# Half the tokens' expert gates by scatter-add into a DRAM grid instead of one-hot matmuls

## The chip, the cores and the metric

The kernel runs on one core of a Trainium2 chip. The metric is the device time of one execution in microseconds, the median of several runs.

## The reference

Two blocks in a row work on 256 tokens of width 1024, all in float32. The first is two layers of sparse attention, short convolution and a squared-ReLU MLP. The second has windowed and neighbourhood attention, and then PEER, the part that the change touches. It retrieves single-neuron experts by product keys:

```python
qh = (xc @ w_query).reshape(PEER_CHUNK, PEER_HEADS, PEER_QDIM)
s1 = einsum('thd,hnd->thn', qh[..., :128], sub_keys[:, 0]); s2 = ... # second half
v1, i1 = top_k(s1, 16); v2, i2 = top_k(s2, 16)
cand = v1[..., :, None] + v2[..., None, :]          # 256 candidates
vs, ci = top_k(cand, 16)
e1 = i1[ci // 16]; e2 = i2[ci % 16]; idx = e1 * 128 + e2
g = softmax(vs)
z = einsum('td,thkd->thk', xc, u_experts[idx])
y = einsum('thk,thkd->td', gelu(z) * g, v_experts[idx])
```

There are 8 heads and 128 x 128 = 16,384 experts.

## The kernel before

The kernel computes PEER densely: it multiplies all 256 tokens by all 16,384 rows of u, masks the gelu with the gates (zero where an expert was not chosen), and multiplies by all rows of v. An expert number is e1 * 128 + e2. A *block* is the 128 experts with one e2; e1 is the partition. The tile `big` (128 partitions x 128 blocks x 256 tokens, 128 KB a partition) holds gelu and gate, first the one and then their product.

A float32 product is made of three float32r products: each weight block is split into a high part (ScalarE, L88) and a low part (VectorE, L89), and TensorE multiplies high by high, high by low and low by high (L117 to L119, L353 to L355). The class `Stream` loads each 512 KB block on SP's queue (L76) into one of three raw buffers, three blocks ahead in PEER (six in the layers), and splits it two blocks ahead (four in the layers).

PEER has three stages:

1. *Up-projection with selection* (L997 to L1009). 24 matmuls per block (`up`, L901); gelu goes into `big` (L911). At blocks 0, 9, ..., 63 a head's query is made with two more weight blocks (`query`, L922), and the generator `select` (L941) takes the scores through top-16, candidates, top-16 and the look-up of e1 and e2 on VectorE. `select` yields after each piece; per block the loop takes SEL_RATE = 1.3 pieces, and three more per query. After all heads the softmax of vs is made and e1, e2 and g are transposed to eT, with tokens along the free dimension (L987 to L991).
2. *Up-projection with gates* (L1038 to L1049). For every four tokens `onehots` makes two 128 x 512 comparisons on VectorE (L1020) and scales the second by g on ScalarE (L1023); `gates` multiplies them on TensorE (L1029, one matmul per token, two records each), which sums the heads and gives 128 x 128 gates of a token. Where gelu is already in `big`, VectorE multiplies it by them (L1031); for the blocks to come ScalarE stores the gates (L1033), and `up` multiplies gelu into them later (L908, L909). The groups of all 256 tokens are spread over the rest of the blocks but the last two (LEAD).
3. *Value* (L1063 to L1079). Pairs of blocks of `big` are split (L124), and 12 matmuls of 512 columns per block add them times v into four PSUM tiles. Then comes the tail, with the residual, the final norm and the output.

The order of the instructions on each engine is planned by the library's scheduler: what is ready goes first, by program order among what is ready, as it reckons the times; `issue_after` and `manual_schedule` fix it by hand. An engine's queue is then worked off in that order, and an instruction that waits holds what is behind it. The DMA queue of SP carries the weights, that of POOL (GpSimd) the small tables, the sub-keys (L924) and row broadcasts (L348). The MLP of the first layer (L659 to L673) is touched too.

Of the kernel before, what the change touches and what calls it, by code (L numbers as in the profile page):

```python
# [9 lines left out]
F32 = mybir.dt.float32  # L10
# [33 lines left out]
GB = 3  # L44
TURN = 1
# [10 lines left out]
SEL_RATE = 1.3  # L56
# [468 lines left out]
def layer(k, l, stream, x, u, rs):  # L525
# [114 lines left out]
    with k.tc.tile_pool(name="mlp", bufs=1, reuse_waits="tile") as mlp:  # L640
# [18 lines left out]
        for j in range(0, HID // P, 2):  # L659
# [52 lines left out]
def ada_steps(k, pool, j0, j1, after):  # L712
# [181 lines left out]
def peer(k, x, pool, hp, stream, u):  # L894
    nc = k.nc
    a = k.a
    with ExitStack() as es:
        eT = pool.tile([P, 3, T], F32, name="eT")
        big = es.enter_context(k.tc.tile_pool(name="bigp", bufs=1, reuse_waits="tile")).tile([P, P, T], F32, name="big")

        def up(e2, done, gl):  # L901
# [4 lines left out]
            if done:  # L906
                g = gl.tile([P, T], F32, name="gl", tag="gl", bufs=2)
                nc.scalar.activation(g[:, :done], ps[:, :done], AF.Gelu_apprx_tanh)  # L908
                nc.vector.tensor_tensor(out=big[:, e2, :done], in0=g[:, :done], in1=big[:, e2, :done], op=ALU.mult)  # L909
            if done < T:  # L910
                nc.scalar.activation(big[:, e2, done:], ps[:, done:], AF.Gelu_apprx_tanh)  # L911
            return end

        e2 = 0
        with k.tc.tile_pool(name="tk", bufs=1, reuse_waits="tile") as tk:
            io16 = tk.tile([P, PK], F32, name="io16")
            nc.gpsimd.dma_start(out=io16, in_=a["iota"][:, :PK])
            vs = [tk.tile([P, H, PK], F32, name=f"vs{t}") for t in range(NT)]
            eg = [tk.tile([P, 3, H * PK], F32, name=f"eg{t}") for t in range(NT)]
# [21 lines left out]
            def select():  # L941
                for h in range(H):
                    while h not in scores:
                        yield
                    s = scores.pop(h)
                    for t in range(NT):
                        v12 = tk.tile([P, 2, PK], F32, name="v12", tag="v12", bufs=2)
                        i12 = tk.tile([P, 2, PK], U32, name="i12", tag="i12", bufs=2)
                        for c in range(2):
                            top16(k, s[:, t, c, :], v12[:, c, :], i12[:, c, :])  # L950
                            yield
                        if12 = tk.tile([P, 2, PK], F32, name="if12", tag="if12", bufs=2)
                        nc.vector.tensor_copy(out=if12, in_=i12)
                        cand = tk.tile([P, PK, PK], F32, name="cand", tag="cand", bufs=1)
                        nc.vector.tensor_tensor(out=cand, in0=v12[:, 0, :, None].to_broadcast([P, PK, PK]),
                                                in1=v12[:, 1, None, :].to_broadcast([P, PK, PK]), op=ALU.add)
                        yield
                        vi = tk.tile([P, PK], U32, name="vi", tag="vi", bufs=2)
                        top16(k, cand.rearrange("p a b -> p (a b)"), vs[t][:, h, :], vi)
                        yield  # L960
                        ab = tk.tile([P, 2, PK], U32, name="ab", tag="ab", bufs=2)
                        nc.vector.tensor_scalar(out=ab[:, 0, :], in0=vi, scalar1=4, scalar2=None,
                                                op0=ALU.logical_shift_right)
                        nc.vector.tensor_scalar(out=ab[:, 1, :], in0=vi, scalar1=15, scalar2=None, op0=ALU.bitwise_and)
                        abf = tk.tile([P, 2, PK], F32, name="abf", tag="abf", bufs=2)
                        nc.vector.tensor_copy(out=abf, in_=ab)
                        for c in range(2):
                            eq = tk.tile([P, PK, PK], F32, name="eq", tag="cand", bufs=1)
                            nc.vector.tensor_tensor(out=eq, in0=abf[:, c, :, None].to_broadcast([P, PK, PK]),
                                                    in1=io16[:, None, :].to_broadcast([P, PK, PK]), op=ALU.is_equal)  # L970
                            nc.vector.tensor_tensor(out=eq, in0=eq, in1=if12[:, c, None, :].to_broadcast([P, PK, PK]),
                                                    op=ALU.mult)
                            nc.vector.tensor_reduce(out=eg[t][:, c, h * PK:(h + 1) * PK], in_=eq, axis=AX.X,
                                                    op=ALU.add)
                            yield
                for t in range(NT):
                    g = eg[t][:, 2, :].rearrange("p (h k) -> p h k", h=H)
                    nc.vector.tensor_tensor(out=g, in0=vs[t], in1=vs[t][:, :, 0:1].to_broadcast([P, H, PK]),
                                            op=ALU.subtract)
                    nc.scalar.activation(g, g, AF.Exp)  # L980
                    den = k.small.tile([P, H], F32, name="den", tag="den")
                    nc.vector.tensor_reduce(out=den, in_=g, axis=AX.X, op=ALU.add)
                    nc.vector.reciprocal(out=den, in_=den)
                    nc.vector.tensor_tensor(out=g, in0=g, in1=den[:, :, None].to_broadcast([P, H, PK]), op=ALU.mult)
                    yield
                    yield
                    ps = k.psm.tile([P, 4, P], F32, name="pst", tag="m")  # L987
                    with k.tc.issue_after(k.end):
                        for c in range(3):
                            nc.tensor.transpose(ps[:, c, :], eg[t][:, c, :], k.ident)  # L990
                    nc.scalar.activation(eT[:, :, t * P:(t + 1) * P], ps[:, 0:3, :], AF.Copy)  # L991
                    yield
# [18 lines left out]
        with k.tc.tile_pool(name="gs", bufs=1, reuse_waits="tile") as gs:  # L1011
            iota = gs.tile([P, P], F32, name="iota")
            nc.gpsimd.dma_start(out=iota, in_=a["iota"])
# [24 lines left out]
            while e2 < P:  # L1038
                upto = min(T, -(-T * (e2 - start + 1) // (P - start - LEAD)))
# [10 lines left out]

            gf = hp.tile([P, 2, D], F32, name="gf", tag="h2hi")
# [30 lines left out]
            xg = gs.tile([P, 512], F32, name="xg", tag="o1", bufs=GB)  # L1082
# [40 lines left out]
def body(tc, a):  # L1123
# [3 lines left out]
    with ExitStack() as es:  # L1127
# [17 lines left out]
        k.t5one = dram.tile([H, 512], F32, name="t5one")  # L1145
        k.ada = keep.tile([P, 48], F32, name="ada")
# [147 lines left out]
```

## Time and profile before

| | |
|---|---|
| median of 3 runs | 1733.88 us (1733.78 to 1741.08) |
| profiled execution | 1734.41 us, span 1732.5 us |
| TensorE busy | 1696.7 us, 98% of the span |
| VectorE, ScalarE, POOL busy | 75%, 52%, 5% |
| moved by DMA | 328.87 MB, 190 GB/s over the span |
| TensorE's granted clock | full in all 40 slices |

A span is the time from the first to the last instruction on the core; the execution's own time has 1.9 us around it. Matmuls overlap, so the mean of one (about 283 ns) is not what one costs; that is read from how many run in a stretch.

### The profile page before, as it was taken

To read this page: it belongs to the slowest core of one execution; us is meant where nothing else is said; L and a number is where in the kernel's file an instruction comes from. 1 tells how busy PE (TensorE), PEld (TensorE's weight loads), DVE (VectorE), ACT (ScalarE), POOL (GpSimd) and SP (SyncE) were. 2 spreads that over 40 slices of the span, in tenths; PEclk is the share of its full clock that TensorE was granted. 3 is DMA by queue.
4 is the path that set the end of the run, shared out by engine and by line. 5 is a ranking of instruction groups with operands and counts; after the bars stand their busy time and mean duration, and the time that the engine had idled before them with its cause. 6 is when DMAs were issued, how large, how long until landed. Compare 5 with 4: busy or idle time off the path is not lost.

```text
span 1732.5 us, 29333 instructions
## 1 busy us (share of the span) xinstructions
PE 1696.7 (98%) x11365; PEld 1557.2 (90%) x11365; DVE 1305.3 (75%) x2131; ACT 902.3 (52%) x1550; POOL 82.3 (5%) x109
## 2 busy tenths in 40 slices
PE   8999999999999999999999999999999999999997
PEld 7899899887999998888789999999999888888886
DVE  6867788766867878767678788799999855555555
ACT  6544544345544544354444444478877644444443
POOL 1000000000000000036100000000000000000000
PEclk9999999999999999999999999999999999999999
DMA  8445667965455659874145655654444566666664
GB/s 309 147 148 183 218 202 242 370 228 195 140 165 183 224 184 318 314 235 150 52 143 181 192 171 185 188 170 123 135 126 124 176 195 190 190 192 193 190 190 131
DMA packets 90778, 328.87 MB, mean 190 GB/s; under 512 B 10384, under 2 KB 10496, under 8 KB 90256
## 3 DMA queue, kind: packets, MB, share of 16 engines
q1 hardware_dynamic: 88144, 318.33, 56.9%
q0 software_dynamic: 2496, 8.68, 1.5%
q8 instruction: 89, 1.46, 0.3%
q14 instruction: 49, 0.40, 0.1%
HBM read 325.88 MB, written 3.19 MB: 190 GB/s over the span
## 4 chain that ended last, share of the span: by engine, by line
PE 90%; DVE 6%; ACT 1%; issue 1%; DMA 1%; SPq 0%; POOLq 0%; POOL 0%; ACTq 0%; DVEq 0%
PE pw L117 15%; PE pw L118 15%; PE pw L119 15%; PE acc L355 13%; PE acc L354 13%; PE acc L353 13%; PE pst L1029 2%; DVE big L1031 2%; DVE wlo L89 1%; DVE o L1020 1%; PE po L473 1%; PE pst L171 1%; PE pst L465 1%; PE sc L812 1%; ACT whi L88 1%
## 5 line engine op out<-in xcount | busy, mean ns | idle before, releaser
L88 ACT ACTIVATE whi<-raw 128x1024 fp32r<-128x1024 f32 (+1 forms) x549 | 572.9, 1048 | 572.8 <-PE pw L118 276.2
L89 DVE TENSOR_TENSOR wlo<-raw,whi 128x1024 fp32r<-128x1024 f32 (+1 forms) x549 | 669.2, 1222 | 253.4 <-ACT whi L88 251.5
L117 PE MATMUL pw<-h2hi,whi 128*128 128x256 f32 x1152 | 331.2, 288 | 0.1
L118 PE MATMUL pw<-h2lo,whi 128*128 128x256 f32 x1152 | 326.0, 283 | 0.3 <-DVE h2lo L178 0.3
L119 PE MATMUL pw<-h2hi,wlo 128*128 128x256 f32 x1152 | 325.8, 283 | 0.0
L117 PE MATMUL pw<-uhi,whi 128*128 128x256 f32 x1000 | 284.9, 285 | 0.0
L119 PE MATMUL pw<-uhi,wlo 128*128 128x256 f32 x1000 | 284.1, 284 | 0.0
L118 PE MATMUL pw<-ulo,whi 128*128 128x256 f32 x1000 | 284.1, 284 | 0.0
L118 PEld LDWEIGHTS pw<-h2lo,whi 128*128 128x128 f32 x1152 | 221.1, 192 | 0.5 <-DVE h2lo L178 0.5
L117 PEld LDWEIGHTS pw<-h2hi,whi 128*128 128x128 f32 x1152 | 220.8, 192 | 0.7 <-ACT big L911 0.5
L119 PEld LDWEIGHTS pw<-h2hi,wlo 128*128 128x128 f32 x1152 | 220.9, 192 | 0.0
L355 PE MATMUL acc<-whi,al 128*128 128x512 f32 x512 | 201.8, 394 | 0.0
L354 PE MATMUL acc<-wlo,ah 128*128 128x512 f32 x512 | 200.7, 392 | 0.0
L353 PE MATMUL acc<-whi,ah 128*128 128x512 f32 x512 | 198.8, 388 | 0.3 <-ACT ah L124 0.3
L118 PEld LDWEIGHTS pw<-ulo,whi 128*128 128x128 f32 x1000 | 192.3, 192 | 1.3 <-issue 1.3
L117 PEld LDWEIGHTS pw<-uhi,whi 128*128 128x128 f32 x1000 | 192.4, 192 | 0.9 <-issue 0.7
L119 PEld LDWEIGHTS pw<-uhi,wlo 128*128 128x128 f32 x1000 | 192.2, 192 | 0.7 <-issue 0.7
L354 PEld LDWEIGHTS acc<-wlo,ah 128*128 128x128 f32 x512 | 96.1, 188 | 22.5
L353 PEld LDWEIGHTS acc<-whi,ah 128*128 128x128 f32 x512 | 96.1, 188 | 21.9 <-ACT ah L124 0.5
L355 PEld LDWEIGHTS acc<-whi,al 128*128 128x128 f32 x512 | 96.3, 188 | 19.5 <-DVE al L124 0.4
L353 PE MATMUL acc<-whi,hhi 128*128 128x512 f32 x256 | 99.9, 390 | 0.0
L354 PE MATMUL acc<-wlo,hhi 128*128 128x512 f32 x256 | 99.8, 390 | 0.0
(253 smaller groups left out, 2495.0 us busy)
## 6 DMA issues: line engine op xcount, KB each, us to landing
raw<-in_w_layers_dram SPq DMA_DIRECT2D x240, 512.0 KB, 4.3
raw<-in_u_dram SPq DMA_DIRECT2D x128, 512.0 KB, 3.7
raw<-in_v_dram SPq DMA_DIRECT2D x128, 512.0 KB, 4.3
aw<-in_w_ada_dram SPq DMA_DIRECT2D x48, 512.0 KB, 5.9
raw<-in_w_query_dram SPq DMA_DIRECT2D x16, 512.0 KB, 3.6
raw<-in_w_qkb_dram SPq DMA_DIRECT2D x8, 512.0 KB, 5.4
raw<-in_w_out_dram SPq DMA_DIRECT2D x8, 512.0 KB, 3.6
raw<-in_w_idx_dram SPq DMA_DIRECT2D x8, 324.0 KB, 6.3
```

Source lines behind the costliest of these rows:

```text
L88: self.nc.scalar.activation(hi[:, :w], r[:, :w], AF.Copy)
L89: self.nc.vector.tensor_sub(lo[:, :w], r[:, :w], hi[:, :w])
L117: nc.tensor.matmul(out, a[0], b[0], start=first, stop=False)
L118: nc.tensor.matmul(out, a[0], b[1], start=False, stop=False)
L119: return nc.tensor.matmul(out, a[1], b[0], start=False, stop=last).ins
L171: k.nc.tensor.transpose(ps[:, c, :], src[:, (c0 + c) * P:(c0 + c + 1) * P], k.ident)
L353: nc.tensor.matmul(acc, a[0], w[0][:, o:o + cols], start=first, stop=False)
L354: nc.tensor.matmul(acc, a[0], w[1][:, o:o + cols], start=False, stop=False)
L355: return nc.tensor.matmul(acc, a[1], w[0][:, o:o + cols], start=False, stop=last).ins
L465: nc.tensor.transpose(ps[:, i, :], sm[:, h, c * P:(c + 1) * P], k.ident)
L1029: nc.tensor.matmul(ps[:, i, :], o1[:, i, :], o2[:, i, :], start=True, stop=True)
L1031: nc.vector.tensor_tensor(out=b[:, :, :cur], in0=ps[:, :, :cur], in1=b[:, :, :cur], op=ALU.mult)
```

## The change

Tokens 0 to 127 keep the one-hot matmuls, now 32 groups of four instead of 64, over the blocks after the selection. For tokens 128 to 255 the gates take another way:

- A DRAM grid `gscr` of 128 x 128 x 128 floats (e1, e2, token; 8.4 MB) is cleared by 16 DRAM-to-DRAM writes of 512 KB, listed one per pair of blocks in the first layer's MLP.
- `select` works on both token tiles at once, makes the softmax after each pair of heads, and works out each gate's place e1 * 16384 + e2 * 128 + token. Then `add_gates` issues 16 indirect DMAs a head from POOL, each adding one gate per token, 128 floats, to the grid. The DMAs of a head don't wait for each other; those of the next head wait for all of them.
- In the value stage `gated_pair` loads the grid four blocks at a time (256 KB, SP) and multiplies a pair of blocks of `big` by it on VectorE, two pairs ahead; the first grid loads wait for the last head's DMAs. The split of a pair is listed one pair ahead, in two buffers instead of three.
- The sub-keys and two tables are loaded on SP's queue instead of POOL's; SEL_RATE is 1.25 instead of 1.3, without the three extra pieces per query.

```diff
+SB = 2
+GQ = 4
+ZERO = 4096
-SEL_RATE = 1.3
+SEL_RATE = 1.25
...
+            if l == 0:
+                clear(k, j // 2, HID // P // 2)
...
+def clear(k, i, n):
+    piece = k.gscr.rearrange("(n r c) o -> n r (c o)", n=n, c=ZERO)[i]
+    k.nc.sync.dma_start(out=piece, in_=k.a["zeros"].to_broadcast(list(piece.shape)))
...
-            if done < T:
-                nc.scalar.activation(big[:, e2, done:], ps[:, done:], AF.Gelu_apprx_tanh)
+            nc.scalar.activation(big[:, e2, done:], ps[:, done:], AF.Gelu_apprx_tanh)
...
+        def add_gates(h):
+            now = []
+            for j in range(PK):
+                ins = nc.gpsimd.indirect_dma_start(
+                    out=k.gscr, out_offset=bass.IndirectOffsetOnAxis(ap=place[:, h, j:j + 1], axis=0),
+                    in_=gate[:, h, j:j + 1], in_offset=None, compute_op=ALU.add).ins
+                k.tc.declare_no_dep(ins, group=f"gates{h}", reason="a head's experts differ, and so do the tokens")
+                k.tc.add_to_no_dep_group(f"gates{h}", ins)
+                for p in added:
+                    k.tc.add_manual_dep(ins, p.name, order, reason="heads add one after the other")
+                now.append(ins)
+            added[:] = now
...
-                keys = tk.tile([P, 2, P], F32, name="keys", tag="keys", bufs=1)
-                nc.gpsimd.dma_start(out=keys, in_=a["sub_keys"][:, 2 * h:2 * h + 2, :])
+                keys = tk.tile([P, 2, P], F32, name="keys", tag="keys", bufs=2)
+                nc.sync.dma_start(out=keys, in_=a["sub_keys"][:, 2 * h:2 * h + 2, :])
...
+                    at = tk.tile([P, PK], F32, name="at", tag="at", bufs=2)
+                    nc.vector.tensor_scalar(out=at, in0=en[:, 1, 1], scalar1=float(P), scalar2=slot, op0=ALU.mult,
+                                            op1=ALU.add)
+                    nc.vector.scalar_tensor_tensor(out=at, in0=en[:, 0, 1], scalar=float(P * P), in1=at, op0=ALU.mult,
+                                                   op1=ALU.add)
+                    nc.vector.tensor_copy(out=place[:, h, :], in_=at)
+                    if h % 2:
...
+                        nc.scalar.activation(e, e, AF.Exp)
...
+                        for i in (h - 1, h):
+                            add_gates(i)
...
-                    due += 3
...
-                upto = min(T, -(-T * (e2 - start + 1) // (P - start - LEAD)))
+                upto = min(P, -(-P * (e2 - start + 1) // (P - start - LEAD)))
...
+            def gated_pair(e0):
+                if e0 % GQ == 0:
+                    g = grids[e0 // GQ] = gs.tile([P, GQ, P], F32, name="gt", tag="gt", bufs=2)
+                    ins = nc.sync.dma_start(out=g, in_=grid[:, e0:e0 + GQ, :]).ins
+                    for p in added:
+                        k.tc.add_manual_dep(ins, p.name, order, reason="all heads have added their gates")
+                b = big[:, e0:e0 + 2, P:]
+                nc.vector.tensor_tensor(out=b, in0=b, in1=grids[e0 // GQ][:, e0 % GQ:e0 % GQ + 2, :], op=ALU.mult)
...
+            gated_pair(0)
+            gated_pair(2)
+            split_pairs = [parts(0)]
             for e0 in range(0, P, 2):
-                ah = gs.tile([P, 2, T], F32R, name="ah", tag="o1", bufs=GB)
-                al = gs.tile([P, 2, T], F32R, name="al", tag="o2", bufs=GB)
-                split(nc, ah, al, big[:, e0:e0 + 2, :])
+                if e0 + 4 < P:
+                    gated_pair(e0 + 4)
+                if e0 + 2 < P:
+                    split_pairs.append(parts(e0 + 2))
+                ah, al = split_pairs.pop(0)
```

## Rows read from the trace of the kernel before

**Rows 1.** The page: busy time of the engines, and the chain that ended last.

```profile
PE 1696.7 (98%) x11365; PEld 1557.2 (90%) x11365; DVE 1305.3 (75%) x2131; ACT 902.3 (52%) x1550; POOL 82.3 (5%) x109
...
PE 90%; DVE 6%; ACT 1%; issue 1%; DMA 1%; SPq 0%; POOLq 0%; POOL 0%; ACTq 0%; DVEq 0%
```

**Rows 2.** Stretches: length, busy and count per engine, granted clock, DMA share, GB/s.

```profile
900.00:1000.00 100.00, 100.00 (x838) 100.00 (x836) 85.56 (x257) 46.81 (x74) 1.61 (x3) 1.00 0.59 179
...
1160.00:1200.00 40.00, 40.00 (x343) 40.00 (x343) 38.97 (x58) 34.18 (x94) 0.00 (x0) 1.00 0.43 131
...
1280.00:1320.00 40.00, 38.56 (x324) 37.98 (x323) 40.00 (x56) 30.35 (x90) 0.00 (x0) 1.00 0.40 123
1320.00:1360.00 40.00, 37.68 (x318) 37.27 (x317) 40.00 (x53) 27.81 (x85) 0.00 (x0) 1.00 0.39 121
...
1400.00:1500.00 100.00, 100.00 (x438) 82.06 (x437) 57.44 (x56) 48.15 (x55) 0.00 (x0) 1.00 0.62 192
```

**Rows 3.** The chain in order of time: start, length, what.

```profile
1152.69 0.33 PE pst L990 x3
...
1163.43 0.89 PE pst L1029 x8
...
1269.12 2.07 DVE big L1031 x2
...
1350.78 1.14 DVE big L1031
```

**Rows 4.** VectorE's groups from 1155 to 1370.

```profile
L1020 DVE TENSOR_TENSOR o<-iota,eT 128x512 f32<-128x512 f32 x128 | 82.6, 693 | 0.9 <-PE pst L1029 0.8
L1031 DVE TENSOR_TENSOR big<-pst,big 128x304 f32<-128x304 f32 (+31 forms) x64 | 68.8, 1095 | 0.3
L89 DVE TENSOR_TENSOR wlo<-raw,whi 128x1024 fp32r<-128x1024 f32 x52 | 63.8, 1226 | 2.1 <-ACT whi L88 2.1
L909 DVE TENSOR_TENSOR big<-gl,big 128x8 f32<-128x8 f32 (+49 forms) x50 | 14.7, 295 | 0.6 <-ACT gl L908 0.6
```

**Rows 5.** ScalarE's groups, shapes kept apart.

```profile
L911 ACT ACTIVATE big<-pw 128x256 f32<-128x256 f32 x76 | 27.9, 367 | 0.0
...
L980 ACT ACT_TABLE_LOAD x2 | 2.6, 1283 | 0.0
```

**Rows 6.** A VectorE group of the selection, 900 to 1100.

```profile
L969 DVE TENSOR_TENSOR eq<-abf,io 128x256 f32<-128x256 f32 x24 | 10.0, 415 | 0.4
```

**Rows 7.** Timelines of POOL and VectorE: start, length, engine, line.

```profile
826.25 2.40 POOL L84 TENSOR_TENSOR raw<-raw,g 128x1024 f32<-128x1024 f32 x1 [1.24 <-DMA raw<-in_w_out_dram]
...
826.64 3.10 DVE L89 TENSOR_TENSOR wlo<-raw,whi 128x1024 fp32r<-128x1024 f32 x1 [0.84 <-ACT whi L88]
...
960.82 0.54 POOL L924 DMA_DIRECT2D keys<-in_sub_keys_dram  x1 [32.02 <-PE sk L936]
...
960.63 1.23 DVE L89 TENSOR_TENSOR wlo<-raw,whi 128x1024 fp32r<-128x1024 f32 x1 [1.65 <-ACT whi L88]
```

**Rows 8.** DMA: a queue's packets, MB, share; issues with KB each, us to landing.

```profile
q0 software_dynamic: 2496, 8.68, 1.5%
...
raw<-in_u_dram SPq DMA_DIRECT2D x128, 512.0 KB, 3.7
raw<-in_v_dram SPq DMA_DIRECT2D x128, 512.0 KB, 4.3
...
t5scr<-t5one SPq DMA_DIRECT2D x1, 2048.0 KB, 10.6
...
keys<-in_sub_keys_dram POOLq DMA_DIRECT2D x8, 128.0 KB, 3.1
```

**Rows 9.** SP's queue in order of time.

```profile
19.34 0.42 SPq L247 DMA_DIRECT2D gB<-in_norm_mlp_dram  x1
...
199.73 1.38 SPq L725 DMA_DIRECT2D aw<-in_w_ada_dram  x3
```

**Rows 10.** A stretch of the first layer's MLP, as Rows 2.

```profile
200.00:220.00 20.00, 20.00 (x167) 19.72 (x166) 17.03 (x25) 16.09 (x25) 1.25 (x3) 1.00 0.91 314
```

More of the change, by code (lines that the diff above doesn't have):

```diff
@@ L897, in peer @@
     with ExitStack() as es:
-        eT = pool.tile([P, 3, T], F32, name="eT")
+        eT = pool.tile([P, 3, P], F32, name="eT")
+        place = pool.tile([P, H, PK], U32, name="place")
+        gate = pool.tile([P, H, PK], F32, name="gate")
         big = es.enter_context(k.tc.tile_pool(name="bigp", bufs=1, reuse_waits="tile")).tile([P, P, T], F32, name="big")
+        grid = k.gscr.rearrange("(p e t) o -> p e (t o)", p=P, t=P)
+        order = mybir.DependencyInfo(mybir.DependencyClass.Sync, mybir.DependencyReason.DATA)
+        added = []
         def up(e2, done, gl):
@@ L951, in select @@
                             yield
[L952 to L956, printed above, removed]
@@ L965, in select @@
[L965 to L975, printed above, removed]
@@ L976, in select @@
[L976 to L984, printed above, removed]
-                    yield
[L986 to L992, printed above, removed]
+                    if12 = tk.tile([P, NT, 2, PK], F32, name="if12", tag="if12", bufs=1)
@@ new lines, in select @@
+                    nc.vector.tensor_copy(out=if12, in_=i12)
+                    cand = tk.tile([P, NT, PK, PK], F32, name="cand", tag="cand", bufs=1)
+                    for t in range(NT):
+                        nc.vector.tensor_tensor(out=cand[:, t], in0=v12[:, t, 0, :, None].to_broadcast([P, PK, PK]),
+                                                in1=v12[:, t, 1, None, :].to_broadcast([P, PK, PK]), op=ALU.add)
+                    yield
+                    if h % 2 == 0:
+                        vs = tk.tile([P, 2, NT, PK], F32, name="vs", tag="vs", bufs=2)
@@ new lines, in select @@
+                    vi = tk.tile([P, NT, PK], U32, name="vi", tag="vi", bufs=2)
+                    for t in range(NT):
+                        top16(k, cand[:, t].rearrange("p a b -> p (a b)"), vs[:, h % 2, t, :], vi[:, t, :])
+                        yield
+                    ab = tk.tile([P, 2, NT, PK], U32, name="ab", tag="ab", bufs=1)
+                    nc.vector.tensor_scalar(out=ab[:, 0], in0=vi, scalar1=4, scalar2=None,
+                                            op0=ALU.logical_shift_right)
@@ new lines, in select @@
+                    nc.vector.tensor_copy(out=place[:, h, :], in_=at)
+                    if h % 2:
+                        n = 2 * NT
+                        g = vs.rearrange("p h t k -> p (h t) k")
+                        ex = tk.tile([P, 2, NT, PK], F32, name="ex", tag="ex", bufs=1)
+                        e = ex.rearrange("p h t k -> p (h t) k")
+                        nc.vector.tensor_tensor(out=e, in0=g, in1=g[:, :, 0:1].to_broadcast([P, n, PK]),
+                                                op=ALU.subtract)
+                        nc.scalar.activation(e, e, AF.Exp)
+                        den = k.small.tile([P, 2, NT], F32, name="den", tag="den")
+                        nc.vector.tensor_reduce(out=den.rearrange("p h t -> p (h t)"), in_=e, axis=AX.X, op=ALU.add)
+                        nc.vector.reciprocal(out=den, in_=den)
+                        yield
+                        for t, dst in ((1, gate), (0, first[:, 2])):
+                            nc.vector.tensor_tensor(out=dst[:, h - 1:h + 1, :], in0=ex[:, :, t, :],
+                                                    in1=den[:, :, t:t + 1].to_broadcast([P, 2, PK]), op=ALU.mult)
+                        for i in (h - 1, h):
+                            add_gates(i)
@@ L994, in peer @@
+                    yield
+                ps = k.psm.tile([P, 4, P], F32, name="pst", tag="m")
+                with k.tc.issue_after(k.end):
+                    for c in range(3):
+                        nc.tensor.transpose(ps[:, c, :], first[:, c].rearrange("p h k -> p (h k)"), k.ident)
+                nc.scalar.activation(eT, ps[:, 0:3, :], AF.Copy)
+                yield
             sel = select()
@@ L1049, in peer @@
                         done = t0 + 4
+        with k.tc.tile_pool(name="vs", bufs=1, reuse_waits="tile") as gs:
             gf = hp.tile([P, 2, D], F32, name="gf", tag="h2hi")
```

50 lines of the change are left out of this document (35 added, 15 removed).

## The prediction, made before the change was run

> **What bounds the kernel now.** I read the page's busy shares and its chain first [rows 1]: TensorE is busy 98% of the span and carries 90% of the chain that ended last; VectorE carries 6%. So a TensorE instruction that is removed is worth its own time, unless another engine takes over where it stood. The change touches the PEER stages, so I cut these into stretches [rows 2]. In 900 to 1000 (expert up-projection with the selection beside it) TensorE runs 838 instructions in 100 us, 0.1193 us each, without a gap; one block of 24 is 2.86 us. In 1160 to 1200 (up-projection with the gates) the mixture runs at 343 per 40 us. In 1280 to 1320 and 1320 to 1360 it drops to 324 and 318, while VectorE is busy 40.00 of 40. In 1400 to 1500 (value) TensorE runs 438 in 100 us, 2.74 us for a block of 12, and VectorE is busy 57.44.
>
> The chain says the same in order of time [rows 3]: from 1269.12 to 1351.9 its pieces are VectorE's (the gate product of L1031, the split of L89, the one-hots of L1020, L909), elsewhere in the stage TensorE's. VectorE's groups between 1155 and 1370 sum to 82.6 + 68.8 + 63.8 + 14.7 = 229.9 us of overlapping busy time in 215 us [rows 4]: there the gates bind VectorE, and TensorE with it.
>
> **The change part by part.** The sum is made against the profiled execution's 1734.4 us (span 1732.5, 1.9 around it); the median of the three runs, 1733.9, is 0.5 us lower.
>
> *Gates removed from TensorE.* Four tokens are 8 instruction records of L1029, 0.89 us on the chain [rows 3], and the piece is the same wherever TensorE is the limit. 32 of the 64 groups go: 32 x 0.89 = 28.5 us. One of the two sets of three transposes goes too: 0.33 us [rows 3].
>
> *Stalls that go.* Against 343 per 40 us, the two slow stretches lack 19 and 25 instructions: 40 x 19/343 + 40 x 25/343 = 2.2 + 2.9 = 5.1 us. They return if VectorE fits. Counting the yields, the selection ends at block 73 (by the same count before, 75, and the trace has 76 full-width blocks up to there [rows 5]). So 55 blocks carry 32 groups: TensorE needs 55 x 2.86 + 28.5 = 186 us. VectorE: 64 one-hots x 0.693 = 44.4, 32 products x 1.095 = 35.0, 55 splits x 1.226 = 67.4, 55 L909 x 0.295 (it averages the width 128 already) = 16.2; together 163, 88% of 186 where it was 107% of 215. The stall goes, and TensorE is late next. Per block L909 and the two gelu pieces stay.
>
> *Selection.* The same top-16 work. Two is_equal and two reductions of 256 columns become one each of 512: 2 x 0.415 [rows 6] against 0.69, the 512-wide one-hot [rows 4], some 0.5 us less a head, and about four small casts and scalings, near 0.17 us each, more. VectorE is at 85% in this stretch [rows 2] and stays there: nothing. The Exp of each head pair costs a table load and one back: 8 instead of 4, at 1.283 us [rows 5]. ScalarE is busy 47% there, and a split is made two blocks (5.7 us) ahead: nothing; without that cover 4 x 1.3 = 5 us.
>
> *Scatter.* 128 indirect DMAs of 128 four-byte descriptors on POOL, 16 a head, each head behind the landing of the one before. The trace has no indirect DMA. The nearest row is the direct one of L924, 0.54 us of POOL [rows 7], 3.1 us to landing [rows 8]. By the yields the first pair is ready in block 18. From there 109 expert blocks, five queries of two blocks each and the gates remain: 119 x 2.86 + 28.5 = 369 us, which hold 128 DMAs at up to 2.88 us each before a grid load can be late. At 0.54 plus one landing per head the whole takes 128 x 0.54 + 8 x 3.1 = 94 us; issued one at a time to landing, 128 x 3.64 = 466 us, 97 us too late. I take the lower (the group is declared independent, so POOL needn't wait inside a head): 0. What queues behind the waits on POOL is only the gf row load for the tail. On SP the first grid load waits for the last head, and behind it stand the loads of v: were it late, TensorE would run dry after three blocks.
> The descriptors also take the DMA engines. The software queue's 2496 packets took 1.5% of 16 engines' span, 0.167 us each [rows 8]; the 16,384 new ones, if as dear as those, would be 171 us per engine, 0.46 of 369 us on top of a share of 0.59 [rows 2]: just over full. Four bytes should cost far less than those 3.5 KB, and a raw u load (3.7 us to landing [rows 8]) is asked for three blocks, 8.6 us, ahead: 0, with the overfull 0.05 x 369 = 18 us as the upper end.
>
> *Clearing the grid.* 16 DRAM-to-DRAM writes of 512 KB on SP's queue, without any input that makes them wait. They need not sit where the loop writes them: SP issues ready loads early. The norm row of layer 0's MLP leaves at 19.34 us, and three w_ada loads at 199.73, ahead of the weights that the program lists before them [rows 9]. So I expect most clears in the first 20 to 60 us, in front of weight loads. 8.4 MB at the 314 GB/s of 200 to 220 [rows 10] is 27 us; at the 10.6 us of the 2 MB copy t5scr [rows 8], 42 us. If all of it came in one piece on TensorE's path, that is the upper end, less the cover: six raw buffers, 6 x 2.74 = 16 us. The row nearest to it is the burst at 199.35, four such loads, 2 MB (one more beside the three), with TensorE busy 20.00 of 20 through it [rows 10]. Four times that burst is more than was shown, so I take 2 us, with 0 and 26 as ends.
>
> *Value stage.* 64 products of 256 columns on VectorE, 0.415 us as the two-input row of that width [rows 6]: per pair of blocks (5.48 us) VectorE goes from 3.15 to 3.56 us. 32 grid loads of 256 KB add 8.4 MB to 192 GB/s x 351 us = 67 MB, so the DMA share goes from 0.62 [rows 2] to about 0.70. A product that waits for its grid blocks the splits behind it on VectorE; but grid buffers are two, freed three pairs earlier, and a split has about two blocks less 2.3 us of room. 0; the upper end is one landing of 4.3 us [rows 8] at the start of the stage. Splitting one pair ahead with two buffers instead of three changes nothing: a buffer comes free with a pair still to go.
>
> *Sum.* 1734.4 - 28.5 - 0.3 - 5.1 + 2 = 1702.5; against the median, **1702 us**.
>
> **A rule that speaks against it.** In the trace a POOL multiply at 826.25, 2.40 us, met the split L89 of VectorE at 826.64, and that took 3.10 us instead of 1.23; the POOL DMA issue at 960.82 met one too, and that took 1.23 [rows 7].
> The Trainium skill (GPSIMD Engine Reference, Key points) says that GpSimd shares its SBUF interfaces with VectorE, and that an instruction with two SBUF inputs contends. By that rule every indirect DMA, whose indices POOL reads from SBUF, could hold a split. The first pair of rows agrees with it, the second shows no cost for a direct issue; no run here shows an indirect one.
>
> **The rivals.**
> *Scatter holds VectorE (slower).* Place: the 32 DMAs after each pair of heads, in a stage where VectorE has 15% free. A pair comes every 20 blocks, 57 us: 8.6 us free. With x us held per DMA, TensorE loses 32x - 8.6 per pair: from x = 0.27 it costs anything, from 0.54 (17.3 - 8.6 = 8.7, four times 35) the gain is gone. At 0.78 (the multiply's share, 1.87 of 2.40 us, of an issue of 1 us) it is 4 x 16.4 = 65 us: 1702 + 65 = 1767. For it: the multiply row. Against: the direct issue row. Chance 0.09.
> *Scatter ends late (slower).* From 2.88 us per DMA on; at 3.64 the first grid load is 97 us late and the value stage starts with it: 1799. For it: a landing takes 3.1 us. Against: the DMAs of a head are free of each other. Chance 0.06.
> *The clears starve the start (still faster).* With half of the upper end, 13 us in place of 2, 1713; with all 26, 1726. For it: the early issue of ready loads; against: the burst that cost nothing. Chance 0.14.
> *It frees no stall.* If VectorE is still the limit somewhere (the fixed order of its instructions lets waits add up), the 5 us stay: 1707. I count it with the forecast.
> *The wait moves into the value stage.* If each product that opens a grid piece waits the whole landing of 4.3 us, VectorE's free 2 x 1.92 us per piece hide 3.84 of it; 32 x 0.46 = 15 us remain: 1717. Against: two grid buffers let the next load leave early. Chance 0.07.
>
> **How the numbers follow.** Forecast, with its own range 1695 to 1709: 0.61; below that 0.03 (more returns than the counted stall). Clears 0.14, grid waits 0.07, the two slower cases 0.15. The range 1694 to 1726 holds the forecast and nearly all of the clears and grid waits, about 0.8. Half a per cent, 8.7 us, is about what a measurement of this kernel can tell from no change: faster means under 1725.2. That is the forecast, what lies below it, and 0.19 of the clears and grid waits: 0.83. Same is 0.05 (the last 0.02 of those, and the scatter holding VectorE by little over 0.5 us); slower is the rest, 0.12.
>
> **What would show it.** Right: L1029 with 256 records instead of 512; VectorE below 90% in the gates' stretch and TensorE without the dip to 318; the value stage at 438 per 100 us; the end of the up-projection some 34 us earlier. L89 near 1.23 us beside POOL's indirect DMAs shows that they hold nothing; the last one's landing before the up-projection's end that they are in time. Wrong: splits above 2 us in the selection stretch, TensorE waiting on VectorE products for the grid, or TensorE gaps before 100 us behind clears.

## The result, and the profile after

The changed kernel takes 1715.7 us (median of 4 runs, 1712.1 to 1718.4) where the kernel before takes 1735.0 beside it: a ratio of 0.988, 95% interval 0.985 to 0.991. That is faster by more than half a per cent, inside the range given (1694 to 1726), but above the forecast's own range (1695 to 1709) and 13.7 us above the forecast: of the 32 us that were expected (1733.9 to 1702) 19 came. The profiled execution took 1715.93 us, its span is 1714.2.

The page of the changed kernel, beside [rows 1] and the software queue's row of [rows 8] (packets, MB, share of 16 engines):

```profile
PE 1670.0 (97%) x11106; PEld 1529.4 (89%) x11106; DVE 1252.1 (73%) x2081; ACT 864.2 (50%) x1399; POOL 318.5 (19%) x227
...
q0 software_dynamic: 20480, 7.63, 4.2%
...
PE 74%; issue 11%; DVE 8%; DMA 5%; ACT 2%; POOL 1%; SPq 0%; POOLq 0%; DVEq 0%; ACTq 0%
```

TensorE has lost 26.7 us of busy time, and the chain that ends last is no longer nine tenths TensorE. The stretches of [rows 2], with two more of the selection between them:

```profile
900.00:1000.00 100.00, 99.35 (x828) 98.94 (x827) 83.90 (x243) 48.37 (x76) 44.86 (x24) 1.00 0.68 181
1000.00:1100.00 100.00, 98.65 (x818) 97.84 (x817) 82.36 (x242) 50.91 (x79) 78.61 (x42) 1.00 0.73 177
1100.00:1200.00 100.00, 97.62 (x802) 97.01 (x800) 80.59 (x175) 60.20 (x126) 80.30 (x45) 0.98 0.69 161
...
1280.00:1320.00 40.00, 40.00 (x340) 40.00 (x339) 32.43 (x46) 25.91 (x69) 0.00 (x0) 1.00 0.51 157
1320.00:1360.00 40.00, 31.41 (x215) 28.88 (x214) 22.28 (x35) 15.16 (x35) 0.61 (x1) 0.87 0.61 188
1400.00:1500.00 100.00, 99.94 (x437) 81.53 (x436) 64.84 (x80) 48.78 (x55) 0.00 (x0) 1.00 0.71 226
```

The gates' stretch is as forecast: 340 instead of 324, VectorE at 81% instead of full. Two places are worse than before. Where the selection runs, TensorE does 828 and 818 instructions per 100 us instead of 838, though VectorE is no busier. And from 1320 to 1360, which now holds the passage to the value stage, it is busy 31.41 of 40 us, at a clock of 0.87.

It helps to cut the time at two marks: the start of the first and of the last up-projection matmul (first start and last start of these lines in each trace). What follows the second mark is taken to the span's end. The expectations below take the end of the last matmul, some 0.2 us later.

| kernel | median us | first up | last up | up stage | after it |
|---|---|---|---|---|---|
| before | 1733.9 | 885.0 | 1370.6 | 485.6 | 361.9 |
| changed | 1715.7 | 880.9 | 1341.5 | 460.6 | 372.7 |
| e4_half_before | 1699.7 | 884.9 | 1338.1 | 453.2 | 361.3 |
| e2_no_scatter | 1716.4 | 880.6 | 1338.5 | 457.9 | 372.3 |
| e3_iota_early | 1715.8 | 885.5 | 1343.3 | 457.8 | 373.1 |
| e5_split_order | 1710.1 | 883.0 | 1336.6 | 453.6 | 372.6 |
| e1_first_grid | 1711.0 | 884.0 | 1341.0 | 457.0 | 368.5 |
| e7_same_pool | 1710.5 | 883.0 | 1343.7 | 460.7 | 365.4 |
| e8_all | 1706.5 | 884.8 | 1338.3 | 453.5 | 366.4 |
| e9_paced | 1699.7 | 884.7 | 1337.0 | 452.3 | 360.9 |

So the up stage won 25.0 us where 33.9 were forecast (28.5 + 0.3 + 5.1), and what follows lost 10.8 where 0 was. The first mark moves by 5 us from execution to execution with the granted clock from 745 to 880 (0.97 in the changed kernel's profile, 0.92 in that of before and of e9_paced; the "full in all 40 slices" of the table ahead is the page's digit 9, which stands for nine tenths or more). e9_paced and e10_twice differ only in how often the scatter is issued, after that mark, and have it at 884.7 and 880.3. It is therefore not put to the change's account, and kernels are compared by the two stages. How far a stage repeats can be seen from the four kernels that pass into the value stage in the same way (changed, e2_no_scatter, e3_iota_early, e5_split_order): 372.3 to 373.1 us after the second mark.

**The passage to the value stage.** SP's queue (start, length, what), then VectorE, in the changed kernel:

```profile
1341.18 0.33 SPq L79 DMA_DIRECT2D raw<-in_v_dram  x1
1341.83 0.33 SPq L1107 DMA_DIRECT2D gf<-in_final_g_dram  x1
1342.47 0.82 SPq L1122 DMA_DIRECT2D gt<-gscr  x2
```

```profile
1343.95 0.28 DVE L927 TENSOR_TENSOR big<-gl,big 128x128 f32<-128x128 f32 x1
1348.80 0.76 DVE L1126 TENSOR_TENSOR big<-big,gt 128x256 f32<-128x256 f32 x2 [4.57 <-DMA gt<-gscr]
```

The first two grid loads leave at 1342.47 and not earlier, although the last scatter was issued at 1244.0. Before them on SP stand five v loads, each waiting for a raw buffer (the first leaves at 1327.98, the last at 1341.18), and the load of final_g, whose tile is one that the up-projection reads to its last matmul at 1341.5. By these rows final_g alone holds the grid back by less than a microsecond; the rest is its place behind the v loads. The product starts 6.3 us after the grid load has left, the split comes behind the product, and TensorE has its one long wait of the trace. The landing is slow too: in e5_split_order, which passes here in the same way, the first two grid loads land after 8.2 us, beside the final_g load and other loads of 512 KB. TensorE's waits:

```profile
PE acc L356 <- ACT ah L127: 8.1, 1, 8.1
PE pw L122 <- DVE wlo L92: 1.8, 4, 0.5
```

**The selection.** VectorE around one dip (start, length, what):

```profile
938.97 1.21 DVE L92 TENSOR_TENSOR wlo<-raw,whi 128x1024 fp32r<-128x1024 f32 x1
940.09 0.17 DVE L998 TENSOR_SCALAR ab<-vi 128x32 uint32<-128x32 uint32 x1
...
940.62 0.69 DVE L1006 TENSOR_TENSOR eq<-abf,io 128x512 f32<-128x512 f32 x1
941.35 0.76 DVE L1011 TENSOR_TENSOR eq<-eq,if 128x256 f32<-128x256 f32 x2
...
944.48 0.67 DVE L1013 TENSOR_REDUCE en<-eq 128x32 f32<-128x512 f32 x1
945.07 2.35 DVE L92 TENSOR_TENSOR wlo<-raw,whi 128x1024 fp32r<-128x1024 f32 x2
```

Between two weight splits, which are wanted every 2.86 us, stand 5.0 us of selection: both halves of the index search for both token tiles, and the softmax of two heads. The longest such stretch in the kernel before, from 900 to 1100, is 3.2 us. The split at 945.07 frees a raw buffer late, SP asks for the next block of u at 946.31, and ScalarE waits 3.1 us for it at 950. Such a run comes with every second head, and TensorE dips behind each (940, 1000 to 1020, 1070 and 1140).

### The profile page after: what moved, and what is told of

Read it like the earlier page. It is cut to its first block, busy times and chain, and to the rows that moved or that the text cites. A ratio compares the mean times of both kernels' runs of the same rounds, so it can differ in the third digit from the quotient of the medians.

```text
span 1714.2 us, 28850 instructions
## 1 busy us (share of the span) xinstructions
PE 1670.0 (97%) x11106; PEld 1529.4 (89%) x11106; DVE 1252.1 (73%) x2081; ACT 864.2 (50%) x1399; POOL 318.5 (19%) x227
## 4 chain that ended last, share of the span: by engine, by line
PE 74%; issue 11%; DVE 8%; DMA 5%; ACT 2%; POOL 1%; SPq 0%; POOLq 0%; DVEq 0%; ACTq 0%
PE pw L122 13%; PE pw L121 13%; PE pw L120 13%; PE acc L358 10%; PE acc L357 10%; PE acc L356 10%; DMA gt<-gscr 3%; DVE wlo L92 2%; PE pst L1082 2%; PE po L476 1%; ACT whi L91 1%; PE pst L174 1%; DVE i L888 0%; PE pst L468 0%; DVE big L1126 0%
## 5 line engine op out<-in xcount | busy, mean ns | idle before, releaser
L935 POOL DMA_INDIRECT gscr<-gate,place x128 | 241.1, 1883 | 127.0 <-DVE first L1036 66.6
```

The source lines that it names most:

```text
L935: ins = nc.gpsimd.indirect_dma_start(out=k.gscr, out_offset=bass.IndirectOffsetOnAxis(ap=place[:, h, j:j + 1], axis=0), in_=gate[:, h, j:j ...
```

## The experiments

**e4_half_before: the removal alone.**

```
-                upto = min(T, -(-T * (e2 - start + 1) // (P - start - LEAD)))
+                upto = min(P, -(-P * (e2 - start + 1) // (P - start - LEAD)))
```

> The kernel before, with only the first 128 tokens gated by one-hot matmuls; the gates of the second half are left out (gelu alone goes into the value stage), nothing of the scatter, the grid, the clears or the new selection is there. It prices the removal alone. Theory: 28.5 us of TensorE and 5.1 us of stall go, up stage 452 us instead of 485.9, time 1734 - 33.6 = 1700 us (1698 to 1703). Rival (the removal itself is worth only the 25 us by which the up stage got shorter): 1708 to 1711 us.

Measured: 1699.7 us (1697.0 to 1701.1), ratio 0.9793 (0.9772 to 0.9813). The first theory holds: the removal is worth 34.3 us. So what the changed kernel lacks, 16 us, was lost by the parts that were added. The intervals of the ratios of e1_first_grid, e5_split_order and e7_same_pool below overlap with the changed kernel's; what they won is read from their stages.

**e2_no_scatter: without the 128 indirect DMAs.**

```
-                        for i in (h - 1, h):
-                            add_gates(i)
```

> The changed kernel without its 128 indirect DMAs: the gates of the second half of the tokens are computed but never added into the grid, so the output leaves them out. Theory (descriptors in the way): the eight waits of ACT for raw u loads between 900 and 1200 (17.8 us) come from the 16,384 four-byte descriptors on the same DMA engines; without them the waits vanish, TensorE runs 836 to 844 instructions per 100 us in 900 to 1200 instead of 828, 818 and 802, and the time falls by 4 to 8 us to 1708 to 1712 us. Rival (the rewritten selection, the keys on SP's queue, the iota load): waits and counts stay within 5 instructions per 100 us and the time at 1714 to 1718 us.

Measured: 1716.4 us (1712.6 to 1716.8), ratio 0.9893 (0.9873 to 0.9913), no change. Its stretches:

```profile
900.00:1000.00 100.00, 99.34 (x828) 98.94 (x828) 83.81 (x246) 49.10 (x77) 0.00 (x0) 1.00 0.57 179
1000.00:1100.00 100.00, 98.68 (x819) 97.87 (x817) 82.29 (x242) 50.96 (x78) 0.00 (x0) 1.00 0.57 177
1100.00:1200.00 100.00, 97.66 (x815) 97.05 (x814) 80.02 (x170) 61.65 (x131) 0.00 (x0) 1.00 0.53 165
```

POOL is empty and the DMA share down from 0.73 to 0.57, but TensorE's counts are the same 828 and 819. (In the third stretch the changed kernel's 802 has the fall of its clock in it, see e3_iota_early.) ScalarE's waits for raw u loads, which were to vanish, are still 14.1 us (17.8 in the changed kernel). My theory, descriptors in the way of the u loads, fell. The gap at the passage stays too (9.7 us): it is no wait for the scatter.

**e5_split_order: the selection's steps kept behind the splits.**

```
-            self.nc.vector.tensor_sub(lo[:, :w], r[:, :w], hi[:, :w])
+            self.cut = self.nc.vector.tensor_sub(lo[:, :w], r[:, :w], hi[:, :w]).ins
...
-                    over = next(sel, True) is True
+                    with k.tc.issue_after(stream.cut):
+                        over = next(sel, True) is True
```

> The changed kernel with one edge more: each step of the selection is put behind the latest weight split on VectorE, so that the order of VectorE's instructions is that of the program and no long run of selection stands between two splits. In the changed kernel and in the one without scatter every second head has such a run (is_equal, products and reductions of both halves, the softmax of two heads: 940.09 to 945.07, 5.0 us) where a split is wanted every 2.86 us; the dips of TensorE follow these runs. Theory (the run holds the split up): no run above 4 us is left, the dips at 940 to 950, 1005 to 1015, 1070 to 1080 and 1135 to 1150 go, TensorE counts 834 to 840 per 100 us in 900 to 1100 (828 and 818 before this), the up-projection takes 455 to 457 us instead of 460.8, the time is 1710 to 1713 us. Rival (VectorE simply has too much to do there, or the keys and raw loads on SP's queue are late): the dips only move, counts within 5 of the changed kernel's, time 1714 to 1718 us.

Measured: 1710.1 us (1708.2 to 1712.4), ratio 0.9866 (0.9848 to 0.9883). The changed kernel, then this one, in the stretch of the run above and (the second line of this one) at a later dip, where the changed kernel has 75:

```profile
940.00:950.00 10.00, 9.35 (x76) 8.94 (x75) 9.09 (x24) 5.42 (x8) 4.65 (x3) 1.00 0.46 126
```

```profile
940.00:950.00 10.00, 10.00 (x86) 10.00 (x85) 9.76 (x24) 6.60 (x10) 0.00 (x0) 1.00 0.53 161
...
1070.00:1080.00 10.00, 10.00 (x86) 10.00 (x85) 9.76 (x21) 6.07 (x9) 8.48 (x6) 1.00 0.78 170
```

Three of the four dips go, counts are 836 and 835 per 100 us from 900 to 1100, the up stage falls from 460.6 to 453.6 us. At the fourth, from 1140 to 1150, 78 instructions stand where there were 76; there TensorE now waits 0.7 us for the transposes at the selection's end. The same work, in the same large instructions and with VectorE busier than in the changed kernel (88% against 84%), but in another order, with at most 3.6 us between two splits from 900 to 1100: it was the run and not the amount. The total alone would not show it; the counts and the stage do. Against e2_no_scatter, e3_iota_early and e1_first_grid (457.9, 457.8 and 457.0), which leave this order alone, the gain is 3.4 to 4.3 us. The changed kernel's own profile has some 3 us more in that stage, with the clock at 0.87 from 1150 to 1160 (below), so I put the price of the order at 3.4 to 4.3 us, and at no more than 7.0.

**e3_iota_early: the iota table loaded before the stage.**

```
+        iota = pool.tile([P, P], F32, name="iota")
+        nc.sync.dma_start(out=iota, in_=a["iota"])
...
-            iota = gs.tile([P, P], F32, name="iota")
-            nc.sync.dma_start(out=iota, in_=a["iota"])
```

> The changed kernel with the iota table in a place of its own, loaded before the PEER stage begins, instead of on SP behind the raw loads at the start of the gates' stage (two small index tiles that VectorE alone uses go from two buffers to one to make room). Theory: the 5.33 us of that load on the chain are a wait of TensorE of about 3 us (window 1155 to 1165: 62 records in 10 us, clock 0.83); the stage starts 2 to 4 us earlier, 1712 to 1714 us. Rival (one-hots and transposes are next late, nothing is won): within 1 us of the changed kernel.

Measured: 1715.8 us (1712.9 to 1721.6), ratio 0.9892 (0.9868 to 0.9916): nothing that can be told. The start of the gates' stage in the changed kernel, in e1_first_grid (which loads iota as the changed kernel does) and here:

```profile
1150.00:1160.00 10.00, 8.36 (x59) 8.15 (x59) 7.13 (x9) 6.44 (x16) 8.48 (x6) 0.87 0.73 172
```

```profile
1150.00:1160.00 10.00, 9.16 (x76) 8.96 (x75) 6.18 (x9) 6.56 (x15) 8.48 (x6) 1.00 0.82 210
```

```profile
1150.00:1160.00 10.00, 9.59 (x78) 9.54 (x79) 8.07 (x14) 5.18 (x12) 8.48 (x6) 1.00 0.83 212
```

The wait for iota is gone, but against e1_first_grid, where the clock stays at 1.00, it was worth 2 instructions of TensorE. The 3 us that I had read from the changed kernel's trace were mostly the fall of the clock to 0.87, which e1_first_grid's profile, with the same load in the same place, does not show. With the selection in e5_split_order's order the load does count a little: from 1150 to 1160 e5_split_order, which loads iota late, has 77 instructions, e8_all and e9_paced, which load it early (among other edits), 87, a difference of 1.2 us.

**e1_first_grid: the first grid load out of its place.** The core of the edit, and the order of split and product exchanged:

```
+                if e2 == P - 16:
+                    with k.tc.issue_after(stream.last):
+                        load_grid(gp, 0, 1)
...
-            gated_pair(0)
-            gated_pair(2)
+            with k.tc.issue_after(k.mul):
+                gated_pair(0)
+                gated_pair(2)
```

> The changed kernel, but the first grid load (256 KB) gets a buffer of its own that exists before the gates' stage ends (one of the o1 buffers pays for it) and goes out on SP 13 expert blocks before the end of the up-projection; the later grid loads stay where they were, and a pair's split is now written ahead of the product of the pair after it. Theory (SP's order): the 8.15 us without a matmul at the start of the value stage are one landing of a grid load that stands on SP behind the final_g load, and that one waits for the last up matmul. Then the gap falls below 2 us, the lower granted clock behind it (0.73 to 0.76 for 20 us) goes with it, and the time is 1716 - 8 to 1716 - 11 = 1705 to 1708 us. Rival (the grid's loads are slow or late for another reason, or the split itself is what is late): the gap stays over 5 us and the time at 1713 to 1718 us.

Measured: 1711.0 us (1709.4 to 1713.7), ratio 0.9864 (0.984 to 0.9889). Half of it: the grid is there, the wait falls from 8.1 to 3.5 us, not below 2. TensorE's wait and VectorE there:

```profile
PE acc L356 <- ACT ah L127: 3.5, 1, 3.5
```

```profile
1343.44 0.28 DVE L927 TENSOR_TENSOR big<-gl,big 128x128 f32<-128x128 f32 x1
1343.65 0.75 DVE L1134 TENSOR_TENSOR big<-big,gt 128x256 f32<-128x256 f32 x2
1344.76 1.29 DVE L127 TENSOR_TENSOR al<-big,ah 128x512 fp32r<-128x512 f32 x2 [0.36 <-ACT ah L127]
```

Products and splits of the first pairs come behind the last block's product; in e4_half_before the first two splits stand at 1333.5, 4.6 us before the last up matmul. Here I had pinned the products behind that block myself, and the value buffers are in a pool of their own.

**e7_same_pool: value buffers in the gates' pool, early grid loads, products free six blocks earlier.**

```
-        with k.tc.tile_pool(name="vs", bufs=1, reuse_waits="tile") as gs:
...
-                ah = gs.tile([P, 2, T], F32R, name="ah", tag="ah", bufs=SB)
-                al = gs.tile([P, 2, T], F32R, name="al", tag="al", bufs=SB)
+                ah = gs.tile([P, 2, T], F32R, name="ah", tag="o1", bufs=GB)
+                al = gs.tile([P, 2, T], F32R, name="al", tag="o2", bufs=GB)
```

> The changed kernel with the value stage's buffers kept in the pool of the gates' stage, as before the change (value splits in the one-hots' buffers, two of each instead of three), the first two grid loads issued 16 and 12 blocks before the end of the up-projection, and the first two grid products put behind a VectorE instruction six blocks before that end. In the run with the early first grid 3.5 us of the gap stayed: the split of the first pair still came after the last product with the gelu. Theory (what is late are two things, the grid load behind final_g on SP, and the value splits, whose new buffers wait for the last up block): both gone, no wait of TensorE above 0.5 us at the start of the value stage, clock 1.00 there, from the last up matmul to the end 361 to 363 us instead of 372.5, time 1716 - 10 to 1716 - 11 = 1705 to 1706 us. Rival (the grid loads and products, now in the up-projection and the first 80 us of the value stage, take VectorE's or the DMA engines' reserve): what is won at the start is lost as TensorE waits for splits later, 1709 to 1716 us.

Measured: 1710.5 us (1709.0 to 1710.9), ratio 0.9866 (0.9851 to 0.9882). The wait on the value split is gone, but others stand in its place:

```profile
PE acc L357 <- DVE wlo L92: 3.0, 5, 1.6
PE pw L122 <- DVE wlo L92: 1.8, 4, 0.5
PE pw L120 <- ACT big L930: 1.8, 5, 0.8
```

What follows the up stage is 7.3 us shorter than in the changed kernel, not 10, and the up stage, with grid products in it, is 3.7 us longer than in e1_first_grid. The rival was right for that: from 1320 to 1400 ScalarE waits 21.4 us in 12 pieces for raw v loads, behind grid loads that go out as soon as a buffer is free.

**e8_all: these edits together (e5, e3, e7).**

> The edits of the runs before together: selection steps behind the splits, the iota table in a place of its own, value buffers in the gates' pool with early grid loads. Theory (three separate stalls, of some 4, 3 and 10 us, add up to what the change fell short of): up-projection 453 to 455 us, from its end to the end of the kernel 361 to 363 us, time 1698 to 1703 us, that is what the removal of the gates alone gave (1699.7 us) plus up to 3 us. Rival (they overlap, or the scatter costs something that shows once the rest is gone): 1704 to 1710 us.

Measured: 1706.5 us (1702.9 to 1706.9), ratio 0.984 (0.9826 to 0.9855): in the rival's range. The up stage is as the theory has it (453.5), what follows is not (366.4). ScalarE and VectorE there:

```profile
1346.53 1.06 ACT L91 ACTIVATE whi<-raw 128x1024 fp32r<-128x1024 f32 x1 [1.98 <-DMA raw<-in_v_dram]
```

```profile
1350.78 0.43 DVE L1133 TENSOR_TENSOR big<-big,gt 128x256 f32<-128x256 f32 x1 [5.51 <-DMA gt<-gscr]
```

**e9_paced: grid loads and products at the pace of the weights.**

```
+                if e0 % GQ == 0 and e0 + 2 * GQ < P:
+                    with k.tc.issue_after(stream.last):
+                        load_grid(e0 + 2 * GQ)
...
+                    with k.tc.issue_after(stream.cut):
+                        gated_pair(e0 + 4)
```

> The kernel with all edits so far, and the grid loads paced: each of the later 30 is put on SP behind the load of the weight block that the program has just asked for, its two products on VectorE behind the latest weight split, and the final_g load moves to the middle of the value stage. In the kernel with all edits the value stage still takes 366.2 us from the last up matmul to the end, where the kernel before takes 361.7: the grid loads go out as fast as buffers come free (all by 1430), ACT waits 1.7 to 2.0 us three times for a raw v load behind them and VectorE 5.5 us for a grid piece. Theory (the burst delays the first v loads): 361.5 to 363 us, TensorE 438 per 100 us from the start, time 1701 to 1703 us. Rival (VectorE's or ACT's own load at the transition holds the splits): 365 to 367 us and 1705 to 1707 us.

Measured: 1699.7 us (1699.5 to 1701.7), ratio 0.9807 (0.9793 to 0.982). The stage after the second mark is 360.9 us, and the time is 1.3 us below the theory's range. The edit paces the grid loads, puts the products behind the splits and moves the final_g load to the middle of the value stage; which of the three gave the 6.8 us against e8_all was not separated. TensorE has one wait left in both stages:

```profile
PE pst L1047 <- DVE den L1036: 0.7, 1, 0.7
```

```profile
1300.00:1340.00 40.00, 40.00 (x328) 39.51 (x327) 31.24 (x43) 23.47 (x60) 0.60 (x1) 1.00 0.55 170
1340.00:1360.00 20.00, 20.00 (x89) 16.43 (x88) 12.25 (x15) 9.89 (x12) 0.00 (x0) 1.00 0.76 240
...
1400.00:1500.00 100.00, 100.00 (x439) 82.04 (x438) 63.03 (x73) 48.13 (x55) 0.00 (x0) 1.00 0.68 216
```

This is the fastest version with all of the computation in it: 16 us below the changed kernel, and level with e4_half_before, which leaves half of the gates out. Scatter, grid, clears and the new selection can thus be had for nothing that is measured (e9_paced also has the early iota load, which e4_half_before has not).

**e10_twice: every indirect DMA issued twice, on e9_paced.**

```
-            for j in range(PK):
+            for j in [*range(PK)] * 2:
```

> The same kernel with every indirect DMA issued twice (256 instead of 128), so that the gates of the second half come out doubled. It asks from where on the scatter decides. By its issue time in the changed kernel (1.88 us and 0.30 us between two) 256 take 558 us from 945 on and end near 1503; the first grid load, which waits for them and stands in front of the weight loads of the last 13 up blocks, is then 200 us late: 1702 + 205 = 1890 to 1920 us, and VectorE's splits stay at 1.2 us. Rival (the issue shrinks or grows with the number in flight, or POOL's issues begin to hold VectorE): an end of the scatter before 1450 or after 1550, or splits above 1.5 us.

Measured, one run: 1910.9 us. The scatter's issues, SP's first grid load behind them, ScalarE's wait, and the splits from 900 to 1240:

```profile
L939 POOL DMA_INDIRECT gscr<-gate,place x256: 1544/1550/2718, 949.9 to 1489.8; - x128
```

```profile
1492.91 0.33 SPq L1094 DMA_DIRECT2D gt<-gscr  x1
```

```profile
ACT whi L91 <- DMA raw<-in_u_dram: 215.0, 1, 215.0
```

```profile
L92 DVE TENSOR_TENSOR wlo<-raw,whi x110: 1194/1219/1254, 901.6 to 1236.3; 128x1024 fp32r<-128x1024 f32 x110
```

256 DMAs take 540 us, 2.1 each with the gap, where 2.18 was expected, and the time is inside the expected 1890 to 1920. The first grid load leaves 201 us later than in e9_paced (1291.5), ahead of weight loads that are then late, and the time is 211 us longer. The splits do not notice.

## Why the prediction came out as it did

The mechanism of the gain was right, and two terms put at nothing were not. That the time is still inside the range is in part luck: the room above 1709 was meant for clears (1713 to 1726) and for 32 small waits for the grid (1717), and neither took place. What filled it was the order of VectorE's instructions in the selection, which was priced at nothing (a rival named waits from a fixed order, but for the gates' stall), and one wait at the start of the value stage, longer than the upper end given for it.

*Gates and stalls off TensorE, 28.5 + 5.1 us: right.* e4_half_before shows 34.3 us in the median and 32.4 in the up stage, 1.5 less than the sum.

*Selection, "the same top-16 work ... stays there: nothing": wrong, by 3.4 to 4.3 us, at most 7.0.* I added durations and found room (VectorE 84% against 85%), and looked at ScalarE's cover, but not at the order: up to 5.0 us of pieces came to stand between two splits, where it had been 3.2 us at most. e5_split_order, with the same instructions, shows that a new order is the cure.

*Scatter, 0: right, though it costs more POOL time than I took.* The nearest row, 0.54 us of a direct issue [rows 7], was too low by a factor of 3 to 4:

```profile
L935 POOL DMA_INDIRECT gscr<-gate,place x128: 1542/1698/3197, 944.7 to 1244.0; - x128
```

The last is issued at 1244, some 100 us before the first grid load; the bound of 2.88 us per DMA was the right question, and 1.88 with a gap of 0.30 is under it. e10_twice shows the other side. The software queue from 900 to 1160 (packets, MB, share of 16 engines):

```profile
q0 software_dynamic: 13058, 0.05, 13.5%
```

0.135 x 260 x 16 / 13,058 is 0.043 us a packet. The 92 indirect DMAs issued in that stretch thus took 35 us of each engine, so by estimate 49 us for all 128 (35 x 128 / 92) and not the 171 that the packet price of [rows 8] gives; and e2_no_scatter shows that they delay nothing that is measured.

*Scatter holds VectorE (rival): refuted.* Beside the indirect DMAs the two-input split takes 1.20 to 1.24 us, as in [rows 7] beside the direct issue and not as beside the multiply:

```profile
L92 DVE TENSOR_TENSOR wlo<-raw,whi x109: 1201/1220/1239, 900.1 to 1239.2; 128x1024 fp32r<-128x1024 f32 x109
```

The Trainium skill (GPSIMD Engine Reference, Key points) would have let them contend on the shared SBUF interfaces; for this instruction no run here agrees.

*Clears, +2: 0.* They are issued one or two at a time from 37 to 232 us, four of the 16 by 60 us where most were expected, and TensorE's count from 50 to 100 us is that of before, with 199 instead of 148 GB/s moved (the kernel before, then the changed one):

```profile
50.00:100.00 50.00, 49.35 (x387) 45.77 (x385) 40.93 (x95) 28.60 (x67) 0.29 (x2) 1.00 0.47 148
```

```profile
50.00:100.00 50.00, 49.34 (x387) 45.78 (x386) 40.96 (x95) 28.37 (x67) 0.29 (x2) 1.00 0.61 199
```

*Value stage, "0; the upper end is one landing of 4.3 us": wrong, by 10.8 us.* The products themselves and 8.4 MB more of loads are free, as the 437 per 100 us and e9_paced show. The start is not. I named what would stand behind the first grid load on SP, the loads of v, but not what stands in front of it: five of these loads, and final_g, released by the last up matmul. To the 6.3 us until the product came the split, so that TensorE stood 8.1 us, and then ran at a lowered clock (last section). e1_first_grid, which takes the grid load out of that place and gives it a buffer of its own, takes more than half of the wait away; which of the loads ahead of it counts was not tested by a run. With the grid in time it still waited 3.5 us for the first split; how much of that is the pool and how much my own pin was not separated. The step "splitting one pair ahead with two buffers instead of three changes nothing" is not refuted by it: e9_paced splits one pair ahead in two buffers, and TensorE waits for none. The rival of 32 small waits for the grid did not happen as such: VectorE waits for it 15 times, 24.1 us, and from 1400 on TensorE does not notice.

The up stage's 8.9 us below are the 1.5 by which the removal gave less than the sum, the 7.0 that e5_split_order takes off the changed kernel's profile (order and clock), and 0.4 left over.

Together: 1702.5 + 8.9 (up stage) + 10.8 (passage) - 2 (clears) - 4.1 (first mark, not the change's) = 1716.1, against 1715.9 of the profiled execution. This divides one execution by its marks, so that it adds up of itself; what shows the causes is the runs.

## What to carry to other kernels

When work is moved to an idle engine, ask not only for its price there, but for every queue in program order what stands in front of the first instruction that needs the result, and what releases that. A stage in which an engine has 15% free has no room for a long run of other work between two instructions that the bound engine waits for: here 3.2 and 3.6 us between two splits cost nothing that shows, and 4.9 to 5.0 us did, at a step of 2.86 us. And loads that may run ahead as far as buffers allow did so here, in front of those that were urgent; e9_paced ties them to the stream that sets the time.

## What had not been expected of the hardware

An indirect DMA of 128 four-byte descriptors with accumulation keeps POOL 1.54 to 3.20 us (1.88 on average), with 0.30 us to the next, against 0.54 for a direct issue. A packet of these takes 0.043 us on a DMA engine, a quarter of that queue's mean packet before (0.167). In the 8.1 us in which TensorE stood at the passage its granted clock fell to the lower of its two levels (1.2 and 2.4 GHz): it is 0.51 from 1345 to 1355, while the first matmul of the value stage comes at 1349.9. So the wait cost more than its length:

```profile
1340.00:1350.00 10.00, 1.85 (x17) 1.65 (x15) 3.55 (x6) 2.35 (x7) 0.61 (x1) 0.76 0.86 301
1350.00:1360.00 10.00, 9.55 (x31) 7.23 (x32) 6.43 (x14) 3.01 (x4) 0.00 (x0) 0.73 0.46 124
```

Ten microseconds hold 31 instructions there, where e9_paced has 45. Around the end of e1_first_grid's wait of 3.5 us the clock was 0.66 from 1345 to 1350 and 1.00 after.
